# A conformer layer with its MLP on one core: the second MLP product in a written order, with a plain product first, and an out projection that is finished tile by tile

## The chip, the core and the metric

The kernel runs on one core of a Trainium2 chip. The core has five engines that each work through a queue of their own: TensorE (PE, matrix products), VectorE (DVE), ScalarE (ACT), GpSimd (POOL) and SyncE (SP), which here only issues DMAs. The metric is the device time of one execution in microseconds; lower is better.

## What is computed

The layer takes x of 512 tokens by 2048 features, in float32:

```
h = rmsnorm(x, norm1_g)
y = conformer_conv(h, ...)          # in projection, gate, 31-tap causal convolution, layernorm, silu, out projection
x = x + y
x = x + square(relu(rmsnorm(x, norm2_g) @ mlp_w1)) @ mlp_w2      # d_ff = 8192
return rmsnorm(x, final_g)
```

The parts that matter here are the end of the conformer's out projection (2048 x 2048), the first MLP product (2048 x 8192), the second (8192 x 2048) and the last norm.

## The kernel before, in words

**Precision.** Each float32 operand is split into a high part (rounded to the matrix format) and a low part (the rest). A product is three matmuls, high x high, low x high, high x low; the helper `mm3` (L349 to L351) issues them. So every weight chunk of 128 x 1024 that is loaded goes through a `make`: a ScalarE copy gives the high part `wh`, a subtraction gives the low part `wl`. The subtraction is done by GpSimd straight from SBUF, or by VectorE, for which ScalarE first copies the high part into a PSUM bank (tag `ax`, two banks).

**The weight stream.** `Stream` holds a list of all chunks in order of use. `get(i)`, called through `chunk()`, makes chunks up to `i + AHEAD` and lets each `make` start the loads of the next `LOAD` items. There are four buffers each for `wh` and `wl`, four `raw` buffers (tag `raw` of the pool `wts`) and eight `rb` buffers in the pool `big`, all of 128 x 1024.

**The conformer's end.** The out projection has 16 output tiles of 128 features in four groups `q` of four; a group accumulates in four PSUM banks over 16 k-tiles, eight weight chunks `c` of two k-tiles each. Beside the matmuls of group `q`, `beside(q, c)` handles the four tiles of the group before: `residual` transposes them on TensorE (L868), copies them to DRAM (`acc`, ScalarE's queue) and squares them with a sum for the norm; `scaled` multiplies by the norm weight; `y_sums` and `pieces` form the operands `y[p, product]` of the first MLP product. In the last group the last four k-tiles go column tile by column tile (L918). Then `evacuate` adds bias and input. This part stands inside `tc.manual_schedule()`: each engine gets its instructions in the order in which they are written.

**The first MLP product** uses seven half-size products instead of eight (a Strassen-Winograd scheme over two token halves and pairs of tiles): for each of 32 pairs `n`, seven products of `FIRST` are accumulated in the banks `X` (`"0"` or `"1"` by turns), `Y` and `Z`, 24 matmuls of 256 columns each. `Squares` applies relu and square, splits the result into `sh` and `sl` and spills both to DRAM, in seven steps beside the next pair's products. The four tiles of the last out projection group get their `residual` in pair 0, in the banks `"1"` and `"Z"`.

**The second MLP product** has eight groups `g` of four pairs, two column halves `q`, and in each the 14 steps of `ORDER`: a product and a k-half `hs`. A step's weight factor is a `Factor`: blocks `11`, `12`, `21`, `22` loaded by SP, differences of them on GpSimd (L166), then the split (L185 to L192). Left operands are the pairs' `ah`, `al`, fetched back from DRAM by `fetch` into seven slots. At the end of a product `add` (L1083) scales the bank by the second norm's factor and adds it to `x2[b, n]`, the residual read back by `stream_back` (L1079). The last group has only its first half in this scheme; the last four k-tiles (pairs 30 and 31) are a plain product at the end, row block `b` by row block, whose weights `w2b` are made in 16 small chunks. This whole part stands outside `manual_schedule`, so a scheduler at build time decides each engine's order. The last norm follows per row block: square sums, a few one-column steps on VectorE, four scalings (L1191) and the store.

## Time and profile before

| what | value |
|---|---|
| median of 3 runs | 1898.04 us (1896.63 to 1898.8) |
| profiled execution, its own time | 1898.16 us |
| its span | 1896.4 us |
| TensorE / VectorE / ScalarE / GpSimd busy | 97% / 66% / 60% / 66% |
| mean granted TensorE clock | 0.988 |
| DMA moved | 323.08 MB, mean 170 GB/s |

The span runs from the first to the last instruction; the execution's own time is 1.8 us longer. Busy time of TensorE counts modelled ends of pipelined matmuls: it says when TensorE had something to do, not that it ran at its fastest pace. The granted clock is the share of full TensorE speed that was allowed; its two levels are 1.2 and 2.4 GHz, so 0.5 and 1.0.

### The profile page before, as it was taken

What the parts mean: (1) busy time and instruction counts of PE and PEld (TensorE: products, weight loads), DVE (VectorE), ACT (ScalarE), POOL (GpSimd) and SP (SyncE); (2) the same over time, 40 slices, a digit from 0 to 9 for tenths busy, and PEclk for the clock granted to TensorE, in tenths of its full rate; (3) what the DMA queues carried; (4) which work ended last, traced back from release to release, by engine and by line L of the source; (5) the groups of instructions that cost most, each with busy time, mean ns of one, the idle gap of its engine ahead of it and who ended that gap; (6) DMA issues with size and microseconds to landing.
All of it is one profiled execution on the core that took longest, in us unless ns stands there. A gap on an engine that the chain in (4) does not pass through costs nothing.

```text
span 1896.4 us, 29173 instructions
## 1 busy us (share of the span) xinstructions
PE 1838.8 (97%) x10866; PEld 1634.9 (86%) x10866; DVE 1254.5 (66%) x1997; ACT 1138.0 (60%) x1770; POOL 1247.4 (66%) x704
## 2 busy tenths in 40 slices
PE   6999999989998999999999999979999999999998
PEld 5888888978887999999999999957888888888876
DVE  8899999994338655555555555526666666666685
ACT  6444444456346666666666666646767776777663
POOL 5699999944433667767767767666566556665643
PEclk9999999999999999999999999989999999999999
DMA  5233333206333455655655655587746647556342
GB/s 213 91 97 96 100 122 100 78 1 220 114 121 122 161 198 186 210 194 181 216 193 179 221 193 179 198 319 275 277 134 232 235 148 271 187 172 237 99 145 100
DMA packets 93165, 323.08 MB, mean 170 GB/s; under 512 B 10336, under 2 KB 10976, under 8 KB 93024
## 3 DMA queue, kind: packets, MB, share of 16 engines
q1 hardware_dynamic: 72432, 258.76, 41.8%
q10 hardware_dynamic: 20592, 62.46, 8.2%
q8 instruction: 85, 1.39, 0.3%
q14 instruction: 56, 0.46, 0.1%
HBM read 255.65 MB, written 65.54 MB: 169 GB/s over the span
## 4 chain that ended last, share of the span: by engine, by line
PE 84%; DVE 7%; DMA 2%; ACT 2%; POOL 2%; issue 1%; SPq 0%; ACTq 0%; DVEq 0%; POOLq 0%
PE mm L350 26%; PE mm L351 26%; PE mm L349 26%; PE mm L727 7%; DVE ax L432 1%; POOL b L166 1%; POOL wl L187 1%; DMA xt<-in_xT 1%; DVE d L616 1%; DVE xl L343 1%; ACT ax L191 0%; DVE y L862 0%; DMA spill<-sl 0%; DVE d L694 0%; DMA acc<-x 0%
## 5 line engine op out<-in xcount | busy, mean ns | idle before, releaser
L349 PE MATMUL mm<-y,wh 128*128 128x256 f32 x1792 | 508.1, 284 | 2.6 <-ACT y L861 2.6
L350 PE MATMUL mm<-y,wh 128*128 128x256 f32 x1792 | 507.6, 283 | 0.1
L351 PE MATMUL mm<-y,wl 128*128 128x256 f32 x1792 | 507.5, 283 | 0.0
L166 POOL TENSOR_TENSOR b<-b,b 128x1024 f32<-128x1024 f32 x120 | 287.7, 2410 | 211.7 <-DMA b<-in_w2s 173.7
L213 POOL TENSOR_TENSOR wl<-b,wh 128x1024 fp32r<-128x1024 f32 x96 | 231.6, 2413 | 212.9 <-ACT wh L212 212.9
L349 PEld LDWEIGHTS mm<-y,wh 128*128 128x128 f32 x1792 | 344.5, 192 | 3.3 <-ACT y L861 2.8
L350 PEld LDWEIGHTS mm<-y,wh 128*128 128x128 f32 x1792 | 344.5, 192 | 0.3 <-DVE y L862 0.3
L351 PEld LDWEIGHTS mm<-y,wl 128*128 128x128 f32 x1792 | 344.4, 192 | 0.0
L350 PE MATMUL mm<-wl,ah 128*128 128x512 f32 x840 | 329.4, 392 | 12.7 <-DVE wl L192 7.9
L349 PE MATMUL mm<-wh,ah 128*128 128x512 f32 x840 | 328.2, 391 | 5.7 <-ACT wh L185 5.1
L351 PE MATMUL mm<-wh,al 128*128 128x512 f32 x840 | 328.5, 391 | 0.0
L192 DVE TENSOR_TENSOR wl<-b,ax 128x512 fp32r<-128x512 f32 x360 | 232.1, 683 | 136.8 <-ACT ax L191 103.8
L185 ACT CAST wh<-b 128x1024 fp32r<-128x1024 f32 x210 | 219.6, 1052 | 164.9 <-PE mm L351 145.0
L133 POOL TENSOR_TENSOR wl<-raw,wh 128x1024 fp32r<-128x1024 f32 x87 | 211.5, 2448 | 104.5 <-ACT wh L132 104.5
L1083 DVE SCALAR_TENSOR_TENSOR acc<-mm,shift,acc 128x512 f32<-128x512 f32 (+1 forms) x241 | 172.1, 745 | 99.2 <-PE mm L351 87.3
L432 DVE SCALAR_TENSOR_TENSOR ax<-u,v,ax 128x512 f32<-128x512 f32 x327 | 218.1, 751 | 0.0
L349 PE MATMUL mm<-xh,wh 128*128 128x512 f32 (+1 forms) x544 | 208.2, 383 | 5.1 <-ACT wh L132 5.1
L351 PE MATMUL mm<-xh,wl 128*128 128x512 f32 (+1 forms) x544 | 207.8, 382 | 3.4 <-DVE wl L133 3.4
L350 PE MATMUL mm<-xl,wh 128*128 128x512 f32 (+1 forms) x544 | 208.3, 383 | 1.3 <-DVE xl L343 1.3
L191 ACT COPY ax<-wh 128x512 f32<-128x512 f32 x360 | 200.3, 585 | 10.8 <-DVE wl L192 7.6
L350 PEld LDWEIGHTS mm<-wl,ah 128*128 128x128 f32 x840 | 158.4, 189 | 48.3 <-DVE wl L192 9.5
L349 PEld LDWEIGHTS mm<-wh,ah 128*128 128x128 f32 x840 | 158.0, 188 | 42.4 <-ACT wh L185 6.4
(203 smaller groups left out, 3021.1 us busy)
## 6 DMA issues: line engine op xcount, KB each, us to landing
b<-in_w1s SPq DMA_DIRECT2D x128, 512.0 KB, 5.0
b<-in_w2s SPq DMA_DIRECT2D x120, 512.0 KB, 4.1
raw<-in_w_in SPq DMA_DIRECT2D x63, 512.0 KB, 3.7
ah<-spill SPq DMA_DIRECT2D x26, 896.0 KB, 7.4
al<-spill SPq DMA_DIRECT2D x26, 896.0 KB, 9.2
raw<-in_w_out SPq DMA_DIRECT2D x32, 512.0 KB, 3.7
spill<-sh ACTq DMA_DIRECT2D x32, 512.0 KB, 7.4
spill<-sl ACTq DMA_DIRECT2D x32, 512.0 KB, 6.2
```

Source lines behind the costliest of these rows:

```text
L133: (nc.vector if sl.stop == cut else self.eng).tensor_tensor(out=lo[:, sl], in0=raw[:, sl], in1=hi[:, sl].bitcast(F32), op=ALU.subtract)
L166: nc.gpsimd.tensor_tensor(out=raw[to, hs], in0=raw[x, hs], in1=raw[y, hs], op=sub)
L185: nc.scalar.copy(out=hi, in_=s)
L191: nc.scalar.copy(out=st, in_=hi[:, sl].bitcast(F32))
L192: nc.vector.tensor_tensor(out=lo[:, sl], in0=s[:, sl], in1=st, op=sub)
L213: nc.gpsimd.tensor_tensor(out=lo, in0=raw[b], in1=hi.bitcast(F32), op=ALU.subtract)
L349: nc.tensor.matmul(out=ps, lhsT=wh, rhs=xh, start=first, stop=False, **how)
L350: nc.tensor.matmul(out=ps, lhsT=wh, rhs=xl, start=False, stop=False, **how)
L351: nc.tensor.matmul(out=ps, lhsT=wl, rhs=xh, start=False, stop=last, **how)
L432: nc.vector.scalar_tensor_tensor(out=o, in0=a, scalar=w, in1=c, op0=ALU.mult, op1=ALU.add)
L727: nc.tensor.matmul(out=ps[n][:, sl], lhsT=a[:, wsl], rhs=x[:, sl], start=first and a is wh and x is hi, stop=last and x is lo)
L1083: nc.vector.scalar_tensor_tensor(out=t, in0=ps, scalar=r2[:, b : b + 1], in1=t, op0=ALU.mult, op1=ALU.add)
```

## The change

- **Out projection.** The weight chunks 5 and 7 of the last group are split by ScalarE and VectorE through PSUM instead of by GpSimd. Residuals are done k-tile by k-tile. In the last four k-tiles each column tile is evacuated and scaled as soon as it is written, and the first three chunks of the MLP are made between them. The last group's residual is done in pairs of tiles and pairs of row blocks, spread over steps 0, 1, 3 and 5 of pair 0, from the pool `prep`.
- **First product.** Pairs 30 and 31 keep their split parts in `rb` and `raw` buffers; pair 30 is not spilled at all. The pool `stage` is closed before the last pair ends, not after.
- **Plain product first.** `Lead` chunks (four, 128 x 1024) hold the weights of pair 30. Right after the first product they are multiplied with pair 30's parts on chip, 96 matmuls; the scaled result starts `x2`. The plain product at the end keeps only pair 31, 96 matmuls.
- **Residual later.** `residual_back` reads a residual tile in steps 2 and 9 of a pass of groups 1 to 6, and GpSimd adds it to `x2` three steps later.
- **Written order.** The second product stands in `manual_schedule()`. `SUM` runs the differences two chunks ahead of the splits, `LOAD` is 5, `AHEAD` 3 instead of 4. The order of steps and of banks is new.
- **Last norm.** Two of the four scalings of a row block go to ScalarE.

The diff, cut to its core:

```diff
-ORDER = [("P1", 0), ("P5", 0), ("P2", 0), ("P1", 1), ("P5", 1), ("P2", 1), ("P6", 0), ("P6", 1), ("P3", 0), ("P3", 1),
-         ("P7", 0), ("P7", 1), ("P4", 0), ("P4", 1)]
+ORDER = [("P1", 0), ("P5", 0), ("P2", 0), ("P1", 1), ("P5", 1), ("P2", 1), ("P6", 0), ("P6", 1), ("P3", 0), ("P7", 0),
+         ("P7", 1), ("P3", 1), ("P4", 0), ("P4", 1)]
...
-FETCH = (((0, 9), (1, 1), (1, 5), (1, 12)), ((0, 2), (0, 6), (0, 10), (1, 12)))
...
+FETCH = ((0, 2), (0, 6), (0, 10), (1, 12))
...
+            if self.eng is None:
+
+                nc.sync.dma_start(out=raw, in_=self.src)
+                nc.scalar.copy(out=hi, in_=raw)
+                for sl in (slice(0, 512), slice(512, 1024)):
+                    st = bank("ax")
+                    nc.scalar.copy(out=st, in_=hi[:, sl].bitcast(F32))
+                    nc.vector.tensor_tensor(out=lo[:, sl], in0=raw[:, sl], in1=st, op=ALU.subtract)
+                return
...
+    class Lead(Plain):
+        raw = None
+        def load(self):
+            if self.raw is None:
+                self.raw = wts.tile([P, 1024], F32, tag="raw", name="raw", bufs=4)
+                nc.sync.dma_start(out=self.raw, in_=self.src)
+        def make(self, hi, lo):
+            nc.scalar.copy(out=hi, in_=self.raw)
+            self.eng.tensor_tensor(out=lo, in0=self.raw, in1=hi.bitcast(F32), op=ALU.subtract)
...
+            while self.summed < min(i + self.SUM + 1, len(self.items)):
+                self.items[self.summed].sum()
+                self.summed += 1
...
-        items += [Plain(w_out[q, c], nc.gpsimd) for c in range(0 if q else 4, 8)]
+        items += [Plain(w_out[q, c], None if q == 3 and c in (5, 7) else nc.gpsimd) for c in range(0 if q else 4, 8)]
...
+    items += [Lead(w2b[0, n], nc.gpsimd) for n in range(4)]
...
+        for i, b in enumerate(rows):
+            sl = slice(i * width, (i + 1) * width)
+            nc.scalar.dma_start(out=acc[b][n][:, tiles[0] % 4 * P :][:, :width], in_=x2[:, sl])
+            k = 5 * b + n + (tiles[0] % 4) // 2
+            nc.scalar.activation(out=sq[:, sl], in_=pt[:, sl], func=AF.Square, accum_out=ss[:, k : k + 1])
...
+            if n == 3:
+                pieces(6, ("P1",))
+                pieces(7, ("P1",))
+            evacuate(12 + n, ps[n])
+            if n < 2:
+                scaled(12 + n, xs[0][:, n * T : (n + 1) * T])
             if n == 0:
-                pieces(5, ("P1", "P2", "P5", "P6", "P7", "P3"))
+                stream.emit()
             elif n == 1:
                 y_sums(6, ("s1", "s2", "s3", "s4"), big)
                 pieces(6, ("P4",))
             elif n == 2:
-                evacuate(14, ps[2])
                 scaled(14, xs[1][:, :T])
                 y_sums(7, ("s3",))
-        pieces(6, ("P1",))
-        pieces(7, ("P1",))
-        evacuate(15, ps[3])
+                stream.emit()
...
+            def home(self, tag, x):
+                if self.n < LASTS:
+                    return stage.tile(list(x.shape), F32R, tag=f"{tag}{x.shape[-1]}", name=tag)
+                pool, t = (big, "rb") if self.n == LASTS else (wts, "raw")
+                return pool.tile(list(x.shape), F32R, tag=t, name=tag, bufs=8 if pool is big else 4)
...
                     if i < 2:
-                        residual(3, 2 * i, banks["1"])
-                        residual(3, 2 * i + 1, banks["Z"])
+                        residual((12, 13), (2 * i, 2 * i + 1), banks["1Z"[i]], prep)
+                        pieces(6 + i, ("P7", "P3"))
                     elif i == 2:
+                        pieces(7, ("P4",))
+                    elif i in (3, 5):
+                        residual((14, 15), (i - 3, i - 2), banks["1"], prep)
...
+        for n in range(4):
+            w = chunk()
+            for b in range(NTOK):
+                ps = bank()
+                for k in range(2):
+                    o = k * T + b * P
+                    mm3(ps, (lead.hi[0][:, o : o + P], lead.lo[:, o : o + P]), tuple(h[:, k * 512 : (k + 1) * 512] for h in w), k == 0, k == 1)
+                x2[b, n] = res.tile([P, 512], F32, name=f"acc{b}{n}")
+                nc.vector.tensor_scalar(out=x2[b, n], in0=ps, scalar1=r2[:, b : b + 1], scalar2=None, op0=ALU.mult)
+            for i in ((0, 1), (2, 3), (5,), ())[n]:
+                before.step(i)
+
+        stream.SUM, stream.LOAD = 2, 5
+        six = [bank() for _ in range(6)]
...
+    def residual_back(step):
+        if step % 7 == 2 and back:
+            b, n = back.pop(0)
+            t = xres.tile([P, 512], F32, name="xb")
+            nc.sync.dma_start(out=t, in_=acc[b][n])
+            waits.append((x2[b, n], t))
+        elif step % 7 == 5 and waits:
+            x, t = waits.pop(0)
+            nc.gpsimd.tensor_tensor(out=x, in0=x, in1=t, op=ALU.add)
...
+        order = "XYZ" if q else "ZYX"
+        banks = {x: six[2 * i : 2 * i + 2] for i, x in enumerate(order)}
...
+            for step in seven(NG - 1, q, 1):
+                if step in (0, 6):
+                    n = 2 * q + step // 6
+                    raw = wts.tile([P, 1024], F32, tag="raw", name="raw", bufs=4)
+                    nc.sync.dma_start(out=raw, in_=w2b[1, n])
+                elif step in (2, 9):
+                    wh, wl = (lasts.tile([P, 1024], F32R, tag=f"{x}{n}", name=x) for x in ("w2h", "w2l"))
+                    nc.scalar.copy(out=wh, in_=raw)
+                    nc.gpsimd.tensor_tensor(out=wl, in0=raw, in1=wh.bitcast(F32), op=ALU.subtract)
...
-            for kk in range(4):
+            for k in range(2):
+                mm3(ps, tuple(x[:, k * T + b * P :][:, :P] for x in a), tuple(x[:, k * 512 + ws.start : k * 512 + ws.stop] for x in wl2[n]), k == 0, k == 1)
...
+                if i < 2:
+                    nc.scalar.activation(out=x3, in_=x3, func=AF.Copy, scale=r)
+                else:
+                    nc.vector.tensor_scalar(out=x3, in0=x3, scalar1=r, scalar2=None, op0=ALU.mult)
```

## Rows read from the trace of the kernel before

**Rows 1.** The page: busy time per engine; busy tenths in 40 slices of the span.

```profile
PE 1838.8 (97%) x10866; PEld 1634.9 (86%) x10866; DVE 1254.5 (66%) x1997; ACT 1138.0 (60%) x1770; POOL 1247.4 (66%) x704
...
PE   6999999989998999999999999979999999999998
```

**Rows 2.** Windows: stretch, length, busy us (instructions) per engine, clock, DMA share, GB/s.

```profile
640.00:1240.00 600.00, 600.00 (x5002) 600.00 (x5001) 331.38 (x563) 386.76 (x625) 421.70 (x266) 1.00 0.58 198
1340.00:1760.00 420.00, 420.00 (x1853) 347.20 (x1852) 270.81 (x420) 300.73 (x420) 263.68 (x111) 1.00 0.61 212
...
578.00:591.00 13.00, 11.63 (x52) 9.04 (x50) 11.91 (x24) 8.38 (x20) 4.77 (x2) 1.00 0.52 195
591.00:612.00 21.00, 14.40 (x103) 13.49 (x103) 13.47 (x30) 15.91 (x38) 3.13 (x2) 0.92 0.29 101
...
1256.00:1281.00 25.00, 11.47 (x30) 7.33 (x31) 5.92 (x10) 8.85 (x13) 11.26 (x5) 0.66 0.95 349
...
1300.00:1320.00 20.00, 18.57 (x81) 14.72 (x80) 7.80 (x13) 9.78 (x14) 19.29 (x9) 1.00 0.88 348
...
1760.00:1780.00 20.00, 19.16 (x85) 15.45 (x84) 8.58 (x14) 10.30 (x15) 17.33 (x8) 1.00 0.17 55
...
1820.00:1845.00 25.00, 23.06 (x98) 17.68 (x97) 24.27 (x34) 15.34 (x24) 12.17 (x8) 1.00 0.42 118
```

**Rows 3.** Timeline of TensorE: start, duration, ..., in brackets idle time before and releaser.

```profile
581.41 0.50 PE L918 MATMUL mm<-vh,wl 128*128 128x512 f32 x1 [1.37 <-POOL wl L133]
...
604.03 0.66 PE L868 MATMUL mm<-ident,xr 128*128 128x128 f32 x4 [2.99 <-ACT sq L873]
...
1272.29 0.80 PE L350 MATMUL mm<-wl,ah 128*128 128x512 f32 x1 [5.96 <-DVE wl L192]
```

**Rows 4.** Timeline of SP's DMA issues across the seam into the second product.

```profile
1254.51 0.38 SPq L150 DMA_DIRECT2D b<-in_w2s  x1
1261.97 0.32 SPq L953 DMA_DIRECT2D ah<-spill  x1
...
1266.19 4.28 SPq L1079 DMA_DIRECT2D acc<-x  x6
```

**Rows 5.** Group of GpSimd's differences: count, busy, mean ns, idle before and releaser.

```profile
L166 POOL TENSOR_TENSOR b<-b,b 128x1024 f32<-128x1024 f32 x120 | 287.7, 2410 | 211.7 <-DMA b<-in_w2s 173.7
```

**Rows 6.** Timeline of VectorE, then of ScalarE, 594 to 604.

```profile
594.07 0.74 DVE L876 SCALAR_TENSOR_TENSOR xr<-mm,v,xr 128x512 f32<-128x512 f32 x1
...
595.60 0.43 DVE L849 TENSOR_TENSOR ysums<-xs 128x256 f32<-128x256 f32 x1 [0.79 <-ACT xs L834]
595.94 0.76 DVE L862 TENSOR_TENSOR y<-xs,y 128x256 fp32r<-128x256 f32 x2
...
602.18 1.29 DVE L223 TENSOR_TENSOR ax<-mm,b 128x512 f32<-128x512 f32 x2
...
600.12 1.06 ACT L217 CAST wh<-mm 128x512 fp32r<-128x512 f32 x2
601.07 1.05 ACT L212 CAST wh<-b 128x1024 fp32r<-128x1024 f32 x1
...
602.28 0.60 ACT L870 COPY x<-mm 128x512 f32<-128x512 f32 x1
...
603.29 0.60 ACT L873 ACTIVATE sq<-mm 128x512 f32<-128x512 f32 x1 [0.40 <-ACT x L870]
```

**Rows 7.** Timeline of VectorE and of GpSimd, 568 to 572.

```profile
569.06 2.51 DVE L847 TENSOR_TENSOR ysums<-ysums,xr 128x256 f32<-128x256 f32 x1
...
568.48 2.80 POOL L133 TENSOR_TENSOR wl<-raw,wh 128x1024 fp32r<-128x1024 f32 x1 [3.69 <-ACT wh L132]
```

**Rows 8.** Timeline of VectorE in the last norm, row block 1.

```profile
1867.91 0.16 DVE L1183 TENSOR_REDUCE r<-ss 128x1 f32<-128x4 f32 x1 [0.79 <-ACT sq L1176]
...
1869.94 2.76 DVE L1191 TENSOR_SCALAR acc<-acc,r 128x512 f32<-128x512 f32 x4
```

**Rows 9.** The page's DMA issues: count, size, median us from issue to landing.

```profile
b<-in_w2s SPq DMA_DIRECT2D x120, 512.0 KB, 4.1
```

More of the change, by code (lines that the diff above doesn't have):

```diff
@@ L1110, in seven @@
                 continue
-            if g == 0 and (q, step) in RESIDUAL:
-                stream_back(*RESIDUAL[q, step])
             w = chunk()
-            part(product, hs, 0, w)
-            waiting.append((product, hs, 1, w))
-            if not (hs == 1 and product in LATE[:-1]):
-                for x in waiting:
-                    part(*x)
-                waiting = []
+            for i in range(2):
+                sl = slice(i * 512, (i + 1) * 512)
+                for s in range(2):
+                    o = LEFT[product] * HT + s * P
+                    left = tuple(y[:, o : o + P] for y in pairs[4 * g + 2 * hs + i])
+                    mm3(banks[BANK[product]][s], left, tuple(y[:, sl] for y in w), product in OPENS and hs == 0 and i == 0,
+                        hs == halves - 1 and i == 1, skip_group_check=True)
@@ L1120, in seven @@
+            if hs == halves - 1:
+                row, col = (int(y) - 1 for y in READS[product])
+                for s in range(2):
+                    add((2 if row == 0 else 0) + s, 2 * q + col, banks[BANK[product]][s])
+            if 0 < g < NG - 1:
+                residual_back(step)
             for p in range(4 if g < NG - 2 else 2 if g == NG - 2 else 0):
[L1121 removed]
+                if (q, step) == FETCH[p]:
                     fetch(4 * g + 4 + p)
[L1124 to L1126 removed]
```

178 lines of the change are left out of this document (72 added, 106 removed).

## The prediction

> **What bounds the kernel now.** I read the page first, for who is busy: TensorE works 97% of the span, so all that can be won without removing matmuls is the rest of it [rows 1]. The slices beside it show where that rest lies: at the start, near 380 to 430 us, near 590, near 1260 and at the end [rows 1]. The change leaves the first two alone. Then I cut the others out with the windows and counted matmuls in them, since a busy share alone cannot tell a pipelined TensorE from one at its peak. In the second MLP product 1853 matmuls of 512 columns take 420 us, 0.2267 us each; in the first 5002 of 256 columns take 600 us, 0.12 us each [rows 2]. Those two paces are TensorE's own: no other engine is over 72% there (ScalarE 300.7 of 420), so the steady parts cannot get faster. What a window lacks against its pace is lost time:
>
> - end of the out projection, 578 to 591: 52 x 0.2267 = 11.8 of 13 us, 1.2 lost
> - seam into the first product, 591 to 612: 87 x 0.12 and 16 transposes at about 0.06 (an estimate: a quarter of the 512 columns' pace) = 11.4 of 21 us, 9.6 lost
> - seam into the second product: 30 x 0.2267 = 6.8 of 25 us and 81 x 0.2267 = 18.4 of 20 us, 18.2 + 1.6 = 19.8 lost
> - last group: 0.7 lost in 1760 to 1780 (85 matmuls) and 2.8 in 1820 to 1845 (98) [rows 2]
>
> The granted clock is 0.66 in the long hole, so 1.2 GHz for most of it, so the hole costs more than its waits [rows 2]. TensorE's timeline names what ended each wait: VectorE for 5.96 us at 1272, ScalarE's square of the residual for 2.99 us at 604, GpSimd's low part of a weight chunk for 1.37 us at 581 [rows 3]. Behind the wait at 1272 stands SP's queue: after 1254.51 it issues nothing until 1261.97, then the residual read-backs go out among the `w2s` loads [rows 4].
>
> **The change part by part.** TensorE's work stays: 64 transposes, and 192 plain matmuls become 96 + 96. So the sum is waits taken away less waits put in, against the profiled execution's 1898.16 us (span 1896.4; the median shown is 1898.04, so one stands for the other).
>
> *Seam into the second product.* `Lead` puts 96 matmuls = 21.8 us between the last product of the first MLP half and the first factor of the second. Their left side is pair 30's own `hi` and `lo`, kept on chip, ready one pair earlier. Their weights are loaded three pieces ahead. Call the end of the first product T. The read-backs of the residual, which stood in SP's queue, are gone from here, and `stage` closes one pair earlier, so pair 31's spill no longer holds the slots. SP then issues in order: four pairs' fetches (7.3 MB), two `Lead` chunks and six blocks (4.2 MB). At the 349 GB/s of the hole [rows 2] 11.5 MB take 33 us; the first fetch can go when P5 of pair 31 is done, five products of 2.9 us or 14 us before T, and the second factor is needed at T + 21.8 + 2.7 = T + 24.5, 38 us later. It fits by 5 us, and the blocks needed first stand in the middle of the queue. The second factor then costs a difference on GpSimd (2.41 [rows 5]), a ScalarE split (1.05), two copies (1.1) and two VectorE pieces (1.3) [rows 6]: under 6 us, beside `Lead`. I take 19.0 of the 19.8 as won and leave 0.8 for a slip; the bounds are all of it and half of it (rival 2).
>
> *Second product in written order.* A factor is made three steps ahead instead of four. A step is 12 matmuls, 2.7 us, so three steps are 8.2 us against a making of 1.05 + 1.1 + 1.3, about 3.5 us [rows 6]. The queues have room: VectorE 271, ScalarE 301, GpSimd 264 of 420 us [rows 2]. The 16 residual adds go to GpSimd, about 1.2 us each (half of [rows 5]'s 2.41): 19 us over 12 passes of 38 us, hidden. `six` and the new `ORDER` leave a step between an evacuation and the bank's next matmul. Cost nothing, hidden under three steps; if a step had to wait for its own factor it would lose 0.8 us (3.5 against 2.7), some 150 us over 13 passes, so the cover must break in only one of them to be seen. The 0.7 lost at 1775 goes (a low part that came late). In the last group the halves of `w2b` are made in whole chunks on GpSimd, not 16 small ones over two engines; of 2.8 us I keep 0.9, since P4 still follows P7 in the same bank and must wait for two evacuations. Won 0.7 + 1.9.
>
> *End of the out projection.* Chunks 5 and 7 of the last column go through PSUM to VectorE instead of GpSimd: the wait at 581 goes, 1.2 won. Each column tile is evacuated as it ends. Call the end of the last tile E. I followed the engine queues in written order with the durations of [rows 6]. Tile 13 ends at E - 5.3; evacuation 0.75, scaling 0.8, four sums and a piece at 0.43: VectorE is free at E - 1.6. Then tile 14's evacuation and scaling, `s3`, P5's four pieces (two low parts, two differences, 0.65 each), two P1 pieces (0.38 each): E + 3.7. The last P1 pieces are needed about E + 2.3 to 2.6: 1.05 us lost. Only then comes tile 15's evacuation: E + 4.45; scaled at E + 5.2, its sums and three pieces by about E + 7. ScalarE then makes P6 (1.1) and P2 (1.05) before it reads out P1 (0.38, a 256-column piece's size): E + 9.45, and P6 writes that same bank, so TensorE, ready at E + 7.9, waits 1.6. Next ScalarE does the first residual: a copy of 0.6, then twice a DMA issue (0.4) and a square of half the width (about 0.35 with its read-out), 2.2 us; then pieces 0.7, P7 1.1, P5's read-out 0.38 and the second residual 2.2: E + 16.0. That one sits in bank Z, which P2 needs; TensorE, ready at E + 12.4, waits 3.7. Together 1.05 + 1.6 + 3.7 = 6.4, and 1.5 for the lower clock and slow transposes, as now (0.92 granted): 7.9 lost against 9.6. Won 1.7, not 9.6: the two residuals of 512 columns each become four half-wide squares with two DMA issues a copy, on the engine that is the bound there. Bounds: a loss of 2.2, if all of ScalarE's added residual work (four times 0.55) shows, and 8.1, if the queues run well ahead and only the clock and transposes remain.
>
> On that stretch the Trainium skill (SBUF — State Buffer, section "SBUF: two separate sides") says that GpSimd and a VectorE instruction with two SBUF inputs take a port pair in turns, each for a whole instruction. The trace bears it out: a sum that takes 0.43 alone took 2.51 us inside a GpSimd piece of 2.80 us [rows 6, 7]. By that rule the chunks moved off GpSimd would give VectorE about 2 us back twice, before E, and speak for the upper bound (rival 1).
>
> *The tail.* The last plain product gives VectorE half as much time per row block: 24 matmuls, 5.4 us. VectorE needs 4 x 0.66 of adding (the scalings' pace), 0.8 of waiting for the last square, 1.4 of small steps (2.03 from the first of them to the first scaling, an addition among them) and now 2 x 0.66 of scaling (two of four go to ScalarE) = 6.2 [rows 8]. Over the blocks it falls some 2.1 us behind, and the end gains about 0.6 from scaling on two engines. I take 1.5 lost; bounds 0 and 2.1.
>
> Sum: 19.0 + 0.7 + 1.9 + 1.2 + 1.7 - 1.5 = 23.0. 1898.2 - 23.0 = **1875.2 us**.
>
> **The rivals.**
>
> 1. The out projection's end is cured: VectorE, spared the port waits, reaches E with no backlog, bank Z is free in time. Against it: the chain through tile 13, 14 and P5's pieces rests on data, not on backlog. For it: a sum of 0.43 us took 2.51 beside a GpSimd piece [rows 6, 7]. Won 8.1 instead of 1.7: 1868.8 us.
> 2. The seam is only half covered: blocks come late behind the fetches, VectorE's pieces of the next factor wait in its queue ahead of `Lead`'s evacuations, and the six banks (8 us) run out. For it: the DMA share is already 0.95 in the hole [rows 2]; 33 us of transfers for 38. It decides when the "12" block lands later than T + 14. About 9 us left instead of 0.8: 1883 us. The Trainium skill (DMA: Bandwidth & Descriptors, section "Queues, rings and completion order") has each DMA engine take descriptors in ring order, so a block waits for the fetches issued before it; the silence of SP in [rows 4] shows the queue's part of it alone.
> 3. Slower: a difference on GpSimd waits in written order for its block, and P2's low part waits behind it, in every pass. A block is issued three steps (8.2 us) before its difference and five (13.6 us) before its difference's last use; with a fetch of 1.8 MB ahead (5.3 us at 349 GB/s) on a transfer of 4.1 us [rows 9] it is 1 us late and still covered. From about 13 us of landing on it costs TensorE time; at 2 us in each of 13 passes, 26 us, it eats more than the gain: 1901 us. For it: GpSimd's differences now wait 173.7 us for these blocks [rows 5]. The automatic order could pull other work forward there, the written one cannot.
> 4. The change does not do what it says: `Lead`'s own weights or pair 30's low part come late and the hole moves ahead of `Lead`. Then some 19 us stay: 1894 us if the rest comes in, 1898 if not. Against it: GpSimd has 2.4 us of work per 2.9 us there.
>
> **How the numbers follow.** My forecast has 0.55, rival 1 0.17, rival 2 0.15, rival 3 0.06, rival 4 0.04; 0.03 for anything else. The likeliest gives 1875. To leave out no more than 2 in 10 the range must take in rival 1 with a full seam and no tail loss, 1868.8 - 0.8 - 1.5 = 1866, and rival 2 with nothing won at E and the tail's other bound, 1883.4 + 2.9 + 0.6 = 1887: 1866 to 1887. Faster by over 0.2% (3.8 us, about what a measurement of this kernel tells from none): 0.90. Within it: 0.03, most of rival 4. Slower: 0.07.
>
> **What would show it.** Right: between the two products no wait of TensorE over 2 us and the granted clock at 1.0; `w2s` issues of SP under `Lead`; about 88 matmuls per 20 us through the second product; two waits of TensorE within 16 us of E, ended by ScalarE's read-out of P1 and by its square. Wrong: a hole of over 5 us at `Lead`; GpSimd's differences waiting with TensorE behind them at each pass; no wait for bank Z (then rival 1).

## The result and the profile after

The changed kernel takes 1875.07 us (median of 4 runs, 1874.4 to 1875.1) against 1898.2 for the kernel before on the same chip: ratio 0.988, 95% interval 0.9865 to 0.9894, 23 us saved. 1875.2 was predicted. The profiled execution has a span of 1873.3 us against 1896.4.

The page of the changed kernel: busy time by engine, then TensorE's and the clock's slices.

```profile
PE 1827.9 (98%) x10860; PEld 1629.8 (87%) x10860; DVE 1254.7 (67%) x2001; ACT 1157.0 (62%) x1782; POOL 1271.5 (68%) x718
...
PE   6999999989999999999999999999999999999996
...
PEclk9999999999999999999999999999999999999998
```

The 7 that stood at 1260 us [rows 1] is a 9, and the last slice has fallen from 8 to 6. Windows of the changed kernel, with the columns of [rows 2]:

```profile
1240.00:1320.00 80.00, 80.00 (x363) 66.62 (x363) 48.60 (x74) 51.38 (x69) 54.12 (x24) 1.00 0.66 252
1340.00:1740.00 400.00, 400.00 (x1766) 331.23 (x1765) 259.99 (x400) 294.81 (x399) 276.49 (x125) 1.00 0.58 225
578.00:590.00 12.00, 12.00 (x62) 10.21 (x61) 8.35 (x19) 6.69 (x15) 2.40 (x1) 1.00 0.49 178
```

TensorE is busy for all of 80 us around the seam into the second product, at full clock. To place the whole saving I took, for each matmul and transpose of both traces, the distance to the next one's start less its pace (0.2267 us for 512 columns, 0.12 for 256, 0.064 for 128 or fewer), and summed the excess by stretch:

| stretch | lost before | lost after | saved | predicted |
|---|---|---|---|---|
| start, 0 to 80 us (untouched) | 21.4 | 22.3 | -0.9 | 0 |
| convolution and norm, 360 to 560 (untouched) | 23.6 | 21.8 | 1.8 | 0 |
| end of the out projection and seam, 580 to 625 | 11.7 | 7.8 | 3.9 | 1.2 + 1.7 |
| seam into the second product, 1230 to 1330 | 21.2 | 0.0 | 21.2 | 19.0 |
| second product, 1330 to 1800 | 1.7 | -0.1 | 1.8 | 0.7 |
| last group and last product | 3.2 | 1.6 | 1.5 | 1.9 |
| start of the last matmul to the end | 8.4 | 14.7 | -6.3 | -1.5 |
| sum | | | 23.0 | 23.0 |

That the time was met to 0.1 us is luck: the tail costs 4.8 us more than predicted, and the seam (2.2), the second product (1.1), the end of the out projection (1.0) and the untouched stretches (0.9) give about as much more. TensorE's timeline of the changed kernel has four waits left behind 580 us, and its last matmul:

```profile
591.47 0.38 PE L380 MATMUL mm<-y,wh 128*128 128x256 f32 x1 [0.85 <-ACT y L892]
593.53 0.58 PE L381 MATMUL mm<-y,wh 128*128 128x256 f32 x1 [1.68 <-DVE y L893]
...
604.81 0.39 PE L380 MATMUL mm<-y,wh 128*128 128x256 f32 x1 [1.10 <-ACT x L912]
...
1814.87 0.47 PE L380 MATMUL mm<-wh,ah 128*128 128x512 f32 x1 [1.25 <-DVE acc L1154]
...
1858.59 0.28 PE L382 MATMUL mm<-w2h,al 128*128 128x256 f32 x1
```

The last norm of the changed kernel, from the timelines of VectorE, ScalarE and GpSimd (L1154 addition, L1230 square, L1232 and L1240 multiplications by the gain, L1237 to L1243 steps to the factor, L1247 and L1249 scalings):

```profile
1857.98 1.64 DVE L1240 TENSOR_TENSOR acc<-acc,fgt 128x512 f32<-128x512 f32 x1
...
1860.27 0.49 DVE L1242 SCALAR_TENSOR_TENSOR r<-r,r 128x1 f32<-128x1 f32 x1
...
1861.15 0.47 DVE L1154 SCALAR_TENSOR_TENSOR acc<-mm,shift,acc 128x256 f32<-128x256 f32 x1
...
1864.71 0.16 DVE L1237 TENSOR_REDUCE r<-ss 128x1 f32<-128x5 f32 x1 [2.30 <-ACT sq L1230]
...
1866.94 1.01 DVE L1249 TENSOR_SCALAR acc<-acc,r 128x256 f32<-128x256 f32 x3
...
1861.32 1.33 ACT L1247 ACTIVATE acc<-acc,r 128x512 f32<-128x512 f32 x2 [2.50 <-DVE r L1243]
1862.57 0.61 ACT L1230 ACTIVATE sq<-acc 128x512 f32<-128x512 f32 x1
...
1856.54 4.21 POOL L1232 TENSOR_TENSOR acc<-acc,fgt 128x512 f32<-128x512 f32 x3 [2.33 <-DVE acc L1154]
```

In the kernel before (TensorE's and VectorE's timelines; L1083 addition, L1183 the sum, L1189 a small step) the last addition came 0.3 us behind the start of the last matmul and the sum 1.1 us behind that:

```profile
1887.96 0.28 PE L351 MATMUL mm<-w2h,al 128*128 128x256 f32 x1
...
1888.27 0.48 DVE L1083 SCALAR_TENSOR_TENSOR acc<-mm,shift,acc 128x256 f32<-128x256 f32 x1 [0.95 <-PE mm L351]
1889.39 0.16 DVE L1183 TENSOR_REDUCE r<-ss 128x1 f32<-128x5 f32 x1 [0.64 <-ACT sq L1176]
...
1890.43 0.16 DVE L1189 SCALAR_TENSOR_TENSOR r<-r,r 128x1 f32<-128x1 f32 x1
```

In the changed kernel TensorE's last matmul starts at 1858.59, yet VectorE makes the last addition at 1861.15. After two scalings it idles 2.30 us, because ScalarE does block 2's scalings, which waited 2.50 us for their factor, before the last block's squares. And VectorE's own multiplication takes 1.64 us beside GpSimd's, where 0.68 is its length alone (in the kernel without multiplications on GpSimd below). Two suspects, then: the queue order and GpSimd.

### The profile page after: what moved, and what is told of

The parts are those of the page before. It is cut to its first block, busy times and chain, and to the rows that moved or that the text cites. A ratio compares the mean times of both kernels' runs of the same rounds, so it can differ in the third digit from the quotient of the medians.

```text
span 1873.3 us, 29336 instructions
## 1 busy us (share of the span) xinstructions
PE 1827.9 (98%) x10860; PEld 1629.8 (87%) x10860; DVE 1254.7 (67%) x2001; ACT 1157.0 (62%) x1782; POOL 1271.5 (68%) x718
## 4 chain that ended last, share of the span: by engine, by line
PE 83%; DVE 12%; ACT 2%; issue 1%; DMA 1%; ACTq 0%; SPq 0%; POOL 0%; DVEq 0%; POOLq 0%
PE mm L380 25%; PE mm L381 25%; PE mm L382 25%; PE mm L758 7%; DVE ax L463 4%; DMA xt<-in_xT 1%; DVE xl L374 1%; DVE d L647 1%; DVE u L421 0%; DVE y L893 0%; DVE d L725 0%; DVE acc L1154 0%; DVE wl L140 0%; PE ax L901 0%; DVE xr L915 0%
## 5 line engine op out<-in xcount | busy, mean ns | idle before, releaser
L140 POOL TENSOR_TENSOR wl<-raw,wh 128x1024 fp32r<-128x1024 f32 x85 | 206.8, 2452 | 103.1 <-ACT wh L139 103.0
L1154 DVE SCALAR_TENSOR_TENSOR acc<-mm,shift,acc 128x512 f32<-128x512 f32 (+1 forms) x241 | 169.6, 743 | 31.6 <-PE mm L382 31.6
L382 PEld LDWEIGHTS mm<-wh,al 128*128 128x128 f32 x840 | 157.7, 188 | 32.7
## 6 DMA issues: line engine op xcount, KB each, us to landing
al<-spill SPq DMA_DIRECT2D x26, 896.0 KB, 10.3
```

The costliest lines, as they stand in the source:

```text
L140: (nc.vector if sl.stop == cut else self.eng).tensor_tensor(out=lo[:, sl], in0=raw[:, sl], in1=hi[:, sl].bitcast(F32), op=ALU.subtract)
L382: nc.tensor.matmul(out=ps, lhsT=wl, rhs=xh, start=False, stop=last, **how)
L1154: nc.vector.scalar_tensor_tensor(out=t, in0=ps, scalar=r2[:, b : b + 1], in1=t, op0=ALU.mult, op1=ALU.add)
```

## The experiments

What each gave, with the excess at the two places and the tail (from the start of the last matmul to the end) by the measure of the table above:

| kernel | us, median (runs) | lost 580 to 625 | lost at the seam | tail |
|---|---|---|---|---|
| changed | 1875.07 (1874.4 to 1875.1) | 7.8 | 0 | 14.7 |
| scalings on VectorE | 1875.98 (1875.4 to 1877.3) | 7.7 | 0 | 16.3 |
| last matmuls twice | 1890.55 (one) | 7.8 | 0 | 9.0 |
| no plain product | 1873.37 (1872.5 to 1876.4) | 7.8 | 19.9 | 14.7 |
| low parts on GpSimd | 1876.23 (1875.2 to 1877.8) | 8.2 | 0 | 14.7 |
| other order at E | 1882.34 (1882.0 to 1884.5) | 14.7 | 0 | 14.7 |
| written last norm | 1875.0 (1874.8 to 1875.5) | 7.7 | 0 | 14.3 |
| automatic second product | 1885.41 (1884.4 to 1888.0) | 7.7 | 4.7 | 14.7 |
| last norm through PSUM | 1870.32 (1868.9 to 1872.7) | 9.3 | 0 | 10.2 |
| no multiplications on GpSimd | 1872.4 (1871.1 to 1874.4) | 7.7 | 0 | 11.5 |
| early read-backs | 1877.04 (one) | 7.7 | 0 | 14.7 |
| residual's bank | 1874.55 (1872.1 to 1876.1) | 6.6 | 0 | 14.7 |
| bank and PSUM | 1870.62 (1869.6 to 1871.9) | 6.7 | 0 | 10.2 |

The 9.3 of the PSUM version is not from an edit: the stretch is the same code. The changed kernel has a granted clock of 0.60 and 0.55 in the two 4 us from 592 to 600 and 1.00 from 605 to 613; the PSUM version has 1.00 in the former and 0.79 in the latter. At full clock it comes to the first product's next parts, P6 and P2, sooner, and waits there for ScalarE (TensorE's timeline):

```profile
599.87 0.39 PE L380 MATMUL mm<-y,wh 128*128 128x256 f32 x1 [1.14 <-ACT four L1083]
...
605.42 0.39 PE L380 MATMUL mm<-y,wh 128*128 128x256 f32 x1 [2.42 <-ACT x L912]
```

The tail of six of the kernels in its parts (starts of instructions in the traces), and what VectorE's instructions took in the last norm beyond their lengths alone (0.22 for a small step, 0.48 for a scaling of 512 columns, 0.68 and 0.42 for a multiplication of 512 and 256):

| kernel | last matmul to last addition | to the last sum | to the first scaling | to the end | VectorE beyond its lengths alone |
|---|---|---|---|---|---|
| before | 0.3 | 1.1 | 1.2 | 5.7 | 3.2 |
| changed | 2.6 | 3.6 | 2.2 | 6.4 | 3.4 |
| scalings on VectorE | 5.7 | 3.1 | 1.2 | 6.2 | 6.4 |
| no multiplications on GpSimd | 0.4 | 3.6 | 1.2 | 6.4 | 0 |
| written last norm | 5.2 | 1.7 | 1.2 | 6.1 | 5.4 |
| last norm through PSUM | 1.5 | 1.1 | 1.3 | 6.3 | 0 |

**Scalings on VectorE.**

```diff
-                if i < 2:
-                    nc.scalar.activation(out=x3, in_=x3, func=AF.Copy, scale=r)
-                else:
-                    nc.vector.tensor_scalar(out=x3, in0=x3, scalar1=r, ...)
+                nc.vector.tensor_scalar(out=x3, in0=x3, scalar1=r, ...)
```

> The changed kernel with one line undone: in the last norm all four scalings of a row block stand on VectorE again, none on ScalarE. The changed kernel's end came 14.7 us behind its last matmul, where the kernel before took 8.4. Theory A: the two ScalarE scalings of a block, which wait for that block's factor (idle times of 1.67, 2.07 and 2.50 us before them), stand in ScalarE's queue ahead of the next block's squares, so that VectorE idles 2.30 us for the last block's sum of squares; without them the last sum comes 1 to 2.4 us earlier, against 0.9 to 1.4 us a block more on VectorE and about 1.5 us more in the last block's scalings: between 1 us shorter and 0.5 us longer, 1874.1 to 1875.6. Theory B: VectorE itself is full, because TensorE now spends only 5.4 us on a block's last product where it spent 10.9: two more scalings in each of four blocks (0.44 to 0.69 us each) all come behind one another, 1876.5 to 1880.

1875.98 us, between the two: 0.9 us slower than the changed kernel. The last sum of squares came 8.8 us behind the last matmul (1868.02 against 1859.20), not earlier. So two scalings on ScalarE are worth about a microsecond. Theory A is not borne out, but the run does not refute the queue order either: with all scalings on VectorE more of its instructions fall beside GpSimd's (6.4 us beyond their lengths alone, 3.4 in the changed kernel), and the last addition comes 5.7 us behind the last matmul instead of 2.6.

**Last matmuls twice.**

```diff
-            for k in range(2):
-                mm3(ps, ..., k == 0, k == 1)
+            for i2 in range(4):
+                k = i2 % 2
+                mm3(ps, ..., i2 == 0, i2 == 3)
```

> The changed kernel with each matmul of the last plain product issued twice into the same sum (the result of that product is doubled), so that TensorE again spends 10.9 us on a row block, as before the change: 96 more matmuls of 0.227 us, 21.8 us. If the tail grew because the halved product no longer covers a block's norm, the end comes 8 to 9 us behind the last matmul and the time is 1875.1 + 21.8 - 6 = about 1891. If the tail grew because of where the scalings stand (ScalarE), it stays near 14 us and the time is about 1896.5.

1890.55 us and a tail of 9.0: the first theory. VectorE's timeline of this kernel, last block (the lines are one further down):

```profile
1881.22 0.16 DVE L1238 TENSOR_REDUCE r<-ss 128x1 f32<-128x5 f32 x1 [0.64 <-ACT sq L1231]
...
1882.01 0.22 DVE L1243 SCALAR_TENSOR_TENSOR r<-r,r 128x1 f32<-128x1 f32 x1
```

The sum comes 1.4 us behind the last matmul (1879.79) instead of 6.1, and the steps have their short durations. The plain product that fills the seam was taken from the end, where it had covered the norm; by this run, a single one, 5.7 us of what the seam gains are paid back there.

**No multiplications on GpSimd.** The next question was which of the two suspects makes the tail.

```diff
-            if i < len(pieces) - 1:
-                nc.gpsimd.tensor_tensor(out=x3, in0=x3, in1=fgt[n][:, ws], op=ALU.mult)
```

> The changed kernel without GpSimd's multiplications by the gain in the last norm (the first three pieces of each block come out without it); VectorE's own multiplication of the last piece stays. Nothing else changes. Theory A (port): VectorE's multiplication falls from 1.14 to 1.64 us to 0.42 to 0.68 and the step beside it from 0.5 to 0.22, so each block's factor comes 1 to 1.3 us earlier and, adding up over the blocks, the tail shrinks from 14.7 to 10 to 12 us: 1870.5 to 1872.5. Theory B (queue order alone: ScalarE's scalings wait for the factor ahead of the next block's squares): GpSimd's work is beside the path, no more than 1 us: 1874 to 1875.

1872.4 us, tail 11.5, as theory A has it. VectorE's timeline, the last norm (two lines up: L1235 is the sum, L1238 the multiplication, L1240 the step):

```profile
1859.46 0.68 DVE L1238 TENSOR_TENSOR acc<-acc,fgt 128x512 f32<-128x512 f32 x1
...
1860.78 0.21 DVE L1240 SCALAR_TENSOR_TENSOR r<-r,r 128x1 f32<-128x1 f32 x1
...
1864.93 0.16 DVE L1235 TENSOR_REDUCE r<-ss 128x1 f32<-128x5 f32 x1 [2.30 <-ACT sq L1230]
```

The durations are short again and the tail is 3.2 us shorter: 2.2 up to the last addition and 1.0 in the last block's small steps. The run takes the multiplications away, not only the waits beside them. The 2.30 us of idle VectorE behind ScalarE's queue have stayed, and with them 2.4 us more than before from the last addition to the last sum. That the order of the queue would give these back is not shown by this run.

**Written last norm.** A block's ending is issued between the next block's pieces; the last norm is in written order.

```diff
+    def ending(b, ss, xs, pieces):
+        ... sum, root          ; yield
+        ... factor             ; yield
+        ... scalings 0, 2      ; yield
+        ... scalings 1, 3
...
-                if i < len(pieces) - 1:
+                if i < 3 + (b == NTOK - 1) or b < NTOK - 1:
                     nc.gpsimd.tensor_tensor(out=x3, in0=x3, in1=fgt[n][:, ws], op=ALU.mult)
                 xs.append(x3)
+                next(end, None)
```

> The changed kernel with the last norm in a written order: the steps that end a row block (sum, root, factor, scalings) are issued between the pieces of the next block, so that no scaling stands ahead of the next block's squares while its factor is missing, and the fourth multiplication of blocks 0 to 2 moves from VectorE to GpSimd. TensorE's work is the same. Theory A: with TensorE's time on a block halved, the 14.7 us behind the last matmul come from the order in the queues and from VectorE's share of the work; then the end comes 9 to 10 us behind the last matmul and the time is 1869.5 to 1870.5. Theory B: three engines are simply too full for 5.4 us a block (GpSimd with four multiplications of 1.27 us has 5.1), in any order: 13 us or more behind the last matmul, 1873.5 or more.

1875.0 us, tail 14.3: theory A missed. This order, with a fourth multiplication on GpSimd, did not cure it. The timelines of VectorE and GpSimd show why (L1225 and L1226 are the two small steps):

```profile
1860.06 0.94 DVE L1225 SCALAR_TENSOR_TENSOR r<-r,r 128x1 f32<-128x1 f32 x1
1861.04 1.19 DVE L1226 SCALAR_TENSOR_TENSOR r<-r,r 128x1 f32<-128x1 f32 x1
...
1859.72 2.49 POOL L1255 TENSOR_TENSOR acc<-acc,fgt 128x512 f32<-128x512 f32 x2 [0.41 <-ACT sq L1253]
```

Steps on one column of 0.22 and 0.16 us last 0.94 and 1.19, the second until GpSimd's multiplication ends at 1862.21. The order did shorten the stretch from the last addition to the last sum, from 3.6 to 1.7 us; but VectorE took 5.4 us beyond its lengths alone instead of 3.4, the additions fell 2.6 us further behind, and what the order won was lost.

**Last norm through PSUM.** The same order; pieces 2 and 3 stay in PSUM, GpSimd has two multiplications, and the small steps take their second operand as a scalar. The cut is against the written last norm.

```diff
-        nc.vector.scalar_tensor_tensor(out=ve, in0=y, scalar=ve, in1=y, op0=ALU.mult, op1=ALU.mult)
-        nc.vector.scalar_tensor_tensor(out=r, in0=ve, scalar=1.5, in1=y, op0=ALU.add, op1=ALU.mult)
+        nc.vector.tensor_scalar(out=ve, in0=y, scalar1=ve, scalar2=y, op0=ALU.mult, op1=ALU.mult)
+        nc.vector.tensor_scalar(out=r, in0=ve, scalar1=1.5, scalar2=y, op0=ALU.add, op1=ALU.mult)
...
-                nc.vector.tensor_scalar(out=xs[i], in0=xs[i], scalar1=r, ...)
+                nc.vector.scalar_tensor_tensor(out=x, in0=xs[i], scalar=r, in1=fgt[n][:, ws], op0=ALU.mult, op1=ALU.mult)
...
+                    x3 = ps
+                    nc.vector.scalar_tensor_tensor(out=ps, in0=ps, scalar=r2[:, b : b + 1], in1=x2[b, n][:, ws], ...)
```

> The changed kernel with the last norm in the written order of the kernel with the ending between the next block's pieces, and in addition with no VectorE instruction there that reads two operands, or a large one, from SBUF alone: pieces 2 and 3 of a block stay in PSUM after the addition and are multiplied by factor and gain in one VectorE instruction from PSUM (like the addition, 0.65 us each), GpSimd multiplies pieces 0 and 1 alone (2 x 1.27 us of 5.4 us a block), and the two small steps of the factor take their second operand as a scalar. VectorE then has 6 x 0.65 + about 0.9 = 4.8 us a block, ScalarE 4.9. Theory A: the tail of 14.7 us comes from VectorE's instructions waiting for GpSimd's port (0.9 to 1.2 us instead of 0.16 to 0.22 for the small steps in the run with the written order, 1.05 and 1.50 instead of 0.47 for scalings): they keep their short durations now, VectorE ends its additions within 1 us of the last matmul, the end comes 8.5 to 10 us behind it, time 1869 to 1870.5. Theory B: the engines are too full whatever the port does: 12 us or more, 1872.5 or more.

1870.32 us, tail 10.2, theory A, a little past its 10. VectorE and GpSimd in the same place:

```profile
1859.41 0.27 DVE L1223 TENSOR_SCALAR r<-r,r 128x1 f32<-128x1 f32 x1
1859.72 0.21 DVE L1224 TENSOR_SCALAR r<-r,r 128x1 f32<-128x1 f32 x1
1859.85 0.75 DVE L1257 SCALAR_TENSOR_TENSOR mm<-mm,shift,acc 128x512 f32<-128x512 f32 x1
...
1863.30 0.16 DVE L1218 TENSOR_REDUCE r<-ss 128x1 f32<-128x5 f32 x1 [0.60 <-ACT sq L1259]
...
1859.07 2.53 POOL L1261 TENSOR_TENSOR acc<-acc,fgt 128x512 f32<-128x512 f32 x2 [2.50 <-ACT sq L1259]
```

Inside GpSimd's 2.53 us the two steps keep 0.27 and 0.21, and the instructions from PSUM 0.75. The last sum comes 2.6 us behind the last matmul. Its runs (1868.9 to 1872.7) lie below all of the changed kernel's, though the two kernels ran in different sets (against the kernel before: 0.9856, interval 0.9841 to 0.9871). No instruction of VectorE in the last norm exceeds its length alone any more, and the last sum comes 1.1 us behind the last addition, as before. Three things moved at once here; their shares were not separated.

**No plain product.**

```diff
-                ps = bank()
-                for k in range(2):
-                    o = k * T + b * P
-                    mm3(ps, (lead.hi[0][:, o : o + P], ...), ..., k == 0, k == 1)
-                nc.vector.tensor_scalar(out=x2[b, n], in0=ps, ...)
+                nc.vector.tensor_scalar(out=x2[b, n], in0=w[0][:, :512].bitcast(F32), ...)
```

> The changed kernel without the matmuls of the plain product of the last but one pair between the two MLP products: its weights are still loaded and split, its sums are filled with a scaled copy of them (so this pair's part of the result is left out), and nothing else moves. 96 matmuls are gone, 21.8 us. Theory A (the prediction's): those matmuls are what hides the loading and splitting of the second product's first weights, and without them TensorE waits some 17 to 20 us there: 1875.1 - 21.8 + 19 = about 1872. Theory B: what cures the wait is the rest (the residual's read-backs no longer ahead of the weights in SyncE's queue, weights loaded six and differences formed three ahead), and the plain product is only work that was put there: a hole of 0 to 8 us, time 1853 to 1861.

1873.37 us: 21.8 us of matmuls are gone and 19.9 us of waits are back. TensorE's timeline of this kernel has them at the first factors of the second product:

```profile
1247.11 0.80 PE L380 MATMUL mm<-wh,ah 128*128 128x512 f32 x1 [5.53 <-ACT wh L207]
...
1268.24 0.80 PE L381 MATMUL mm<-wl,ah 128*128 128x512 f32 x1 [3.46 <-DVE wl L214]
```

Theory A: the plain product is the cover. This kernel still loads and splits that product's weights, so what the rest of the change would save by itself is not shown; beside that work it saved 1.3 of 21.2.

**Early read-backs.**

```diff
-            if 0 < g < NG - 1:
+            if g < NG - 1:
                 residual_back(step)
```

> The changed kernel with the residual's read-backs (16 of 256 KB on SyncE, each added by GpSimd) begun in the first group of the second product instead of the second group. The fetches of the pairs and the second product's weights fill the DMA engines there (401 GB/s, share 1.01). Theory A: what cured the wait at this place is that the read-backs are out of SyncE's queue in front of the weights, as well as the plain product; with them back in the first group TensorE waits 2 us or more there, time above 1877. Theory B: the plain product alone covers it, and one read-back in seven steps is lost among the rest: no wait of more than 0.3 us in the first group, 1874.5 to 1876.

The single time, 1877.04, would fit A, but the windows decide for B; TensorE has no gap at all there:

```profile
1240.00:1320.00 80.00, 80.00 (x372) 66.96 (x372) 47.05 (x72) 50.49 (x67) 56.69 (x26) 1.00 0.69 270
```

The extra time is in the untouched stretch from 360 to 560, where this execution lost 24.5 us against 21.8 (last section). Read-backs in the first group, one in seven steps, cost nothing once the plain product is there. Six in a row ahead of the weights, as in [rows 4], no run shows.

**Automatic second product.**

```diff
-    with tc.manual_schedule():
+    if True:
         for g in range(NG - 1):
```

> The changed kernel with the second MLP product in automatic order again instead of the written one, nothing else changed. By the prediction the written order is worth the late low part (0.7 us, 1.2 in the trace) and part of the last group's waits (1.9, 1.5 in the trace): 1877.5. Rival: it is worth nothing, the waits went with the bank order and the plain product, 1875.1. Another rival: the automatic order sets the residual's additions or the differences ahead of weights that TensorE waits for, more than 5 us, above 1880.

1885.41 us, the third case: 10.3 us slower. 4.7 are lost at 1321 (a wait of 2.9 and a granted clock of 0.79 in the 8 us behind it) and 5.6 more in the last group. The timelines of TensorE, GpSimd and ScalarE of this kernel:

```profile
1321.07 0.50 PE L381 MATMUL mm<-wl,ah 128*128 128x512 f32 x1 [2.75 <-POOL wl L209]
...
1822.55 0.76 PE L380 MATMUL mm<-wh,ah 128*128 128x512 f32 x1 [4.74 <-DVE acc L1154]
...
1313.81 2.54 POOL L1150 TENSOR_TENSOR acc<-acc,xb 128x512 f32<-128x512 f32 x2
...
1318.65 2.36 POOL L209 TENSOR_TENSOR wl<-b,wh 128x1024 fp32r<-128x1024 f32 x1
...
1817.74 1.04 ACT L1205 CAST w2h<-raw 128x1024 fp32r<-128x1024 f32 x1 [5.86 <-DMA raw<-in_w2b]
```

The automatic order sets two of the residual's additions on GpSimd ahead of P2's low part, and a split of the last product's weights, whose transfer has not landed, ahead of the last group's on ScalarE. The additions did not stand there in the kernel before. The written order is what makes the new work free.

**Low parts on GpSimd.**

```diff
-    ... Plain(w_out[q, c], None if q == 3 and c in (5, 7) else nc.gpsimd)
+    ... Plain(w_out[q, c], nc.gpsimd)
```

> The changed kernel with two weight blocks of the out projection's last column (c = 5 and 7) split as in the kernel before: low part in one piece on GpSimd instead of two halves on VectorE through a copy in PSUM. The prediction gave this part 1.2 us: TensorE's wait at the last column comes back, 1876.3. Rival: GpSimd has time now, since the column ends by tiles and the automatic order's work is placed otherwise, 1875.1. Another: VectorE is freed of 2 x 1.3 us beside the pieces of the last tiles, and the time is up to 1 us shorter, 1874.

1876.23 us, inconclusive by the time. TensorE's timeline has the wait back at a fifth of its size:

```profile
581.74 0.50 PE L958 MATMUL mm<-vh,wl 128*128 128x512 f32 x1 [0.27 <-POOL wl L140]
```

0.27 us against 1.37 [rows 3], 0.4 against 1.5 in lost time. Most of the 1.2 us had gone with something else that moved at that column; with what, no run here tells.

**Other order at E.** The split of the second weight block is issued after tile 12 instead of after tile 14; the sums are made where they are used.

```diff
             if n == 0:
                 stream.emit()
-            elif n == 1:
-                y_sums(6, ("s1", "s2", "s3", "s4"), big)
-                pieces(6, ("P4",))
             elif n == 2:
...
+                pieces(6, ("P1",))
+            evacuate(12 + n, ps[n])
...
+            if n == 0:
                 stream.emit()
+            elif n == 2:
+                pieces(7, ("P1",))
+                y_sums(6, ("s1",), big)
+                pieces(6, ("P5",))
```

> The changed kernel with the steps at the end of the out projection in another order: the split of the second weight block of the first MLP product (2.57 us of VectorE, which stood ahead of the last two row tiles' parts for P1) is put forward into VectorE's idle time between the tiles' evacuations, and of the sums only those that P1 and P5 need stand ahead. Theory A: the waits of 1.01 and 1.94 us in P1 come from that split standing in front, and not from VectorE's amount of work (it idled about 4 us of the 9 before), so they go: 2 to 3 us, 1872 to 1873. Theory B: VectorE is full from 590 to 600 us in any order, and what P1 no longer waits for, P5, P6 or P2 waits for: 0 to 1 us, 1874 to 1875.

1882.34 us, 7 slower: both theories missed. The waits in P1 did shrink (to 0.55), but TensorE then waited at P6 and P2. TensorE's timeline, then a sum of VectorE's and a weight block's low part on GpSimd:

```profile
601.33 0.58 PE L380 MATMUL mm<-y,wh 128*128 128x256 f32 x1 [4.54 <-ACT four L1085]
...
609.98 0.38 PE L380 MATMUL mm<-y,wh 128*128 128x256 f32 x1 [3.16 <-ACT x L912]
...
601.20 2.60 DVE L882 TENSOR_TENSOR ysums<-xs,ysums 128x256 f32<-128x256 f32 x1
...
601.09 2.42 POOL L238 TENSOR_TENSOR wl<-b,wh 128x1024 fp32r<-128x1024 f32 x1 [17.61 <-ACT wh L237]
```

Made one after another, sums, ScalarE parts and VectorE parts wait for each other: ScalarE idles 0.55 to 1.20 us before each of four such parts. And a sum of 0.42 us took 2.60 beside GpSimd; ScalarE then waited 2.94 us for VectorE ahead of the residual that P2 waits for, so not all of P2's wait is the order's. The order of the change is the better of the two; whether another order removes the 2.9 us left in P1 is open.

**Residual's bank.**

```diff
-                        residual((12, 13), (2 * i, 2 * i + 1), banks["1Z"[i]], prep)
+                    if i in (0, 2):
+                        residual((12, 13), (i, i + 1), banks["1"], prep)
```

> The changed kernel with one residual read-out at the end of the out projection moved: the transposes of tiles 12 and 13 for row blocks 2 and 3 come after P6 into the bank where those for blocks 0 and 1 were, instead of after P5 into P2's bank. Theory A (the prediction's reading of this wait): P2's first matmul waits (1.26 us lost in the changed kernel) only for ScalarE's squares in its own bank, so the wait goes and nothing takes its place: 1873.8. Theory B: ScalarE is behind by its amount of work there, and the same 1 to 1.5 us come back at the next transposes, which then wait for that bank, or at P7's parts: 1875.

P2's wait is gone from the trace, and 1.1 us of lost time with it (7.79 to 6.65), nothing in its place: theory A. The time, 1874.55 with runs from 1872.1 to 1876.1, cannot show so little.

**Bank and PSUM.** The two diffs that helped, together.

> The changed kernel with that move and with the last norm through PSUM in the written order (which took 1870.3 us with a tail of 10.2 us instead of 14.7). The two places are 1200 us apart and share no work, so the gains add. Theory A: 1870.3 - 1.3 = 1869.0. Theory B: the move gives nothing, 1870.3. In both cases below the changed kernel's 1875.1, and the last norm's part of it is the larger.

1870.62 us (1869.6 to 1871.9): the tail is 10.2 again, the wait in P2 is absent again, and the time is that of the PSUM version alone. This version and that one beat both kernels, by about 4.5 us the changed one; the bank's share stays below what the times resolve.

## Why the prediction was right, and where it was not

- *Seam into the second product, 19.0.* Right in cause: the run without the plain product gets 19.9 us of waits back. Right size 21.2: the 0.8 held back for a slip was not needed, and the lost time counted beyond the two windows of [rows 2] is 21.2, not 19.8. What the queue argument (read-backs ahead of the weights) is worth is not shown: the early read-backs cost nothing, but they came one in seven steps. Blocks land later, 6.7 us median against 4.1 [rows 9], with no wait of TensorE at the seam: rivals 2 and 4 are out.
- *Written order, cost nothing.* Held; rival 3 is out, since GpSimd's differences idle less, not more, than in [rows 5] (the page of the changed kernel):

```profile
L187 POOL TENSOR_TENSOR b<-b,b 128x1024 f32<-128x1024 f32 x120 | 286.8, 2413 | 47.9 <-DVE wl L214 33.9
```

  Its worth was underrated: 0.7 + 1.9 were its two terms (1.8 and 1.5 by the table), but against the automatic order of the same work it is worth 10 us.
- *End of the out projection, 1.2 + 1.7.* 3.9 came. The forecast of 7.9 us still lost at the seam met 7.8 lost over 580 to 625, by luck: 1.05 in P1, 1.6 at P6, 3.7 at P2 and 1.5 of clock and transposes were forecast, and 2.95, 0, 1.3 and 3.6 came. E, the end of the last tile, is 588.30 in the changed kernel. Its timelines of VectorE and ScalarE (L248 a weight block's difference, L915 the evacuation of tile 14, L893 the parts for P1, L912 the second residual's last square):

```profile
584.10 1.30 DVE L248 TENSOR_TENSOR ax<-mm,b 128x512 f32<-128x512 f32 x2 [2.21 <-ACT mm L253]
...
588.65 0.75 DVE L915 SCALAR_TENSOR_TENSOR xr<-mm,v,xr 128x512 f32<-128x512 f32 x1
...
593.05 0.75 DVE L893 TENSOR_TENSOR y<-xs,y 128x256 fp32r<-128x256 f32 x2
...
604.56 0.19 ACT L912 ACTIVATION_READ_ACCUMULATOR x<-mm 128x1 f32 x1
```

  VectorE came to tile 14's evacuation at E + 0.35 and not at E - 1.6, since a weight block's difference that waited 2.21 us for ScalarE stands ahead of tile 13's. The forecast had followed VectorE's queue without the weight blocks' splits in it. So P1 lost 2.95 us (1.01 + 1.94), not 1.05. ScalarE was done with the second residual at E + 16.4, as forecast (E + 16.0), but TensorE, late from P1 and the lower clock (0.60 and 0.55 from 592 to 600), came to P6 and P2 later: P6's 1.6 did not appear, and P2 lost 1.3 instead of 3.7. In the PSUM version, with full clock there, both waits appear, with 1.3 and 2.6 lost. The run with the bank moved shows P2's cause as named. That there was a wait for bank Z keeps rival 1 out; and with the two chunks back on GpSimd the stretch loses 0.4 us more, not 2 us twice.
- *The tail, -1.5 with bounds 0 and 2.1.* This is the term that failed: 6.3. By its parts the 2.1 us "behind" came true in size (2.2 more up to the last addition), though not in cause. What the term put at nothing is 2.4 us from there to the last sum, the squares that ScalarE takes up behind block 2's scalings, and 1.0 us of small steps beside GpSimd; and "the end gains about 0.6 from scaling on two engines" is 0.6 lost from the first scaling to the end, the cause of which stays open. The run without multiplications on GpSimd takes the 2.2 and the 1.0 away, so the backlog is not VectorE's amount of work, as "VectorE needs ... 6.2" had it, but its waits beside GpSimd. The kernel before had as much of them, 3.2 us: its four scalings [rows 8] hold one that took 1.57 where 0.48 is its length alone (VectorE's timeline of the kernel before):

```profile
1870.74 1.57 DVE L1191 TENSOR_SCALAR acc<-acc,r 128x512 f32<-128x512 f32 x1
```

  With 10.9 us a block they cost nothing, with 5.4 they do. The prediction used the port argument at the out projection and not here, where GpSimd is busy 3.8 us or more of each block. That the order would give back the 2.4 is not shown alone: the PSUM version, which changes order, operands and GpSimd's share together, does.
- *Untouched code.* 0.9 us of the 23 came from stretches that the change leaves alone; that is the spread between executions, below.

## What to carry to other kernels

Work moved into a hole is taken from where it stood: price what it covered there, with the shorter time per step, not only what it fills. When a stage's time per step halves, waits between engines that cost nothing while a step had time to spare begin to cost time; a mean duration from the slower stage hides them. A written order is worth what the automatic one would do with the new work, not what it did with the old.

## What was not expected of the hardware

VectorE's small steps lose as much beside GpSimd as large instructions: one column with two SBUF tensors takes 0.94 and 1.19 us instead of 0.22 and 0.16, and the same arithmetic with the second operand as a per-partition scalar takes 0.27 and 0.21 inside a GpSimd multiplication of the PSUM version. Additions of 512 columns from PSUM took 0.72 to 0.76 in either case. The Trainium skill (SBUF — State Buffer, section "SBUF: two separate sides") gives the port pair to whichever instruction starts first, for all of it, against VectorE with two SBUF inputs; the traces agree (the step of 1.19 us ends 0.02 us behind the multiplication that had started first), and two steps whose operand of one column is passed as a scalar did not wait. A scaling of 512 columns, with one tensor, did wait (1.57 above against 0.48).

The untouched code from 360 to 560 us lost between 21.6 and 24.6 us in the executions seen. The granted clock in it differs. The windows of the changed kernel and of the one with low parts on GpSimd, the same code at the same time:

```profile
416.00:432.00 16.00, 15.02 (x120) 14.48 (x120) 12.04 (x39) 13.34 (x26) 4.60 (x6) 1.00 0.13 41
```

```profile
416.00:432.00 16.00, 15.47 (x100) 15.07 (x101) 9.88 (x32) 11.39 (x22) 3.45 (x5) 0.79 0.01 3
```

In one TensorE keeps 2.4 GHz, in the other it has 1.2 GHz for some 6.7 of the 16 us ((1 - 0.79) x 16 / 0.5, an estimate), after a wait of 2.9 us of TensorE at 416 in both. One execution's time therefore says nothing about 2 us; the excess by stretch does.
